# The tail of a PEER layer: another order of its tiles, partial sums kept on chip, and finer steps of routing

## The chip, the cores and the metric

The kernel runs on one core of one Trainium2 chip. The metric is the device time of one execution in microseconds (us). The times of three runs and one profiled execution are given; all rows come from the profiled one.

## What the kernel computes

The reference is one decoder block for 1024 tokens of width 1024: two gated branches and an output projection (dense matmuls), and then PEER, a mixer over 16384 experts of one neuron each. Only the second part matters here, cut from the reference:

```
q = einsum('btd,dq->btq', h, w_q).reshape(B, T, 8, 2, 128)
v1, i1 = top_k(q[..., 0, :] @ keys1.T, 16)
v2, i2 = top_k(q[..., 1, :] @ keys2.T, 16)
...
top_s, pos = top_k(v1 + v2 of all 16 x 16 pairs, 16)
idx = (i1 * 128 + i2) at pos
g = softmax(top_s)
a = gelu(sum over d of h * expert_down[idx])
y = sum over the 8 heads and 16 entries of g * a * expert_up[idx]
```

The block's output is x + gate2 * y, normalised.

## The kernel before, in words

**Halves and blocks.** The tokens are worked in two halves of 512, and the expert part in eight blocks `b` of 128 tokens: 0 to 3 are half 1, 4 to 7 half 2. For each half the dense groups (`group`, `stream`) run first; at its end come the output projection (`w_out_part`) and the four quarters of the query projection (`w_q`). Each quarter `q` gives the scores of two heads, their best eight entries (`s_part`, `tops`) and the number of each head's best expert (`rank`, L1463).

**Routing.** `route` (L317) makes the gates and expert numbers of one quarter; `gates` (L202) is its softmax. `pack_half` (L284) joins a half's quarters into a list in memory, `tsh_d` (written at L312 and L313). `rare` (L367) picks out the few (token, head) pairs that need more than eight entries and builds one extra list for each half, called block 8 or 9 (`NBLK`, `NBLK + 1`). These three are generators. They stand in the queue `qr`, and each `pump` runs one of them to its next `yield`. In the dense part `step()` pumps `qr` by `rate["r"]` for every k step of a group. In the tail, one pump goes with each expert tile.

**Expert tiles.** A tile is 128 gathered rows of the table `tab`, each 2048 numbers: an expert's down and up vectors. There are two kinds.

- A best-entry tile, (b, j) with j from 0 to 7, holds the best expert of head j for each of the 128 tokens of block b. It needs no list, only `dix` of its quarter. `direct_list` (L487) gathers it, `direct_dot` (L491) multiplies it by the block's rows h2 on VectorE and makes a diagonal weight `Wd`.
- A list tile, j from 8 to 17, holds 128 entries of the block's list. `entry_list` (L500) selects them with two matmuls on `th` and `tl` (the list read back at L477 and L478, `load_block`) and gathers the rows (L483). `entry_dot` (L529) brings h2 to the entries by matmuls with `hh` and `hl`, the two halves of a split of h2 (L472, L473), and makes the weight `W`.

Both end in `add_rows` (L552), which sums the tile into the accumulator `acc` of its block: two matmuls, four pieces in the trace (L556). Item j = 18, the rare row (`rare_rows`, L569), adds the block's share of the rare list's result, which went to memory as `yr_d` (`rare_keep`, L577) and is loaded again for each block. `finish` (L595) loads x2, adds and normalises. The blocks of half 1 have their best entries summed elsewhere (`direct_rows`).

**Order.** `peer_stream` (L693) writes out the list `todo` of all 132 items by calls of `seg`. In half 2 it is:

```
for b, n in EARLY:                      # (5, 4), (6, 4), (7, 8)
    seg(b, range(n))
seg(BH, range(last - AH), False)        # block 4, j = 0 to 10
seg(NBLK + 1, range(PH, PH + NTR[1]))   # rare list of half 2, 6 tiles
todo.extend((BH, j) for j in range(last - AH, last + 1))
...
for b in range(BH + 1, NBLK):           # blocks 5, 6, 7: what is left
    seg(b, range(done.get(b, 0), last + 1))
```

The heads of 5, 6 and 7 are interrupted sums: `rows_keep` (L687) writes them to memory (`y_d`), and `finish` loads and adds them. For each item, `fill` gathers up to `ahead` items further on, `dots` makes the product of the next item, and the item's sum follows. In the dense part (stage 1, one pool in `use`, `ahead` 2) the queue `qp` gives `peer_stream` 0.42 to 0.65 of an item per step. In the tail (two pools, `ahead` 7, nine buffers of gathered rows) it runs item after item. A scheduler then orders each engine's instructions; the order of `todo` is their priority.

**Buffers.** `peer_pools` (L435) takes the number of buffers of `hh` and `hl` as `hb`: 1 in the dense part and 2 in the tail. `rowp` holds three rows of 4 KB in each partition. Two accumulators, `pa` and `pa1`, exist in the tail. h2 rows of half 2 go through two buffers (`load_h2`, L456).

Of the kernel before, what the change touches and what calls it, by code (L numbers as in the profile page):

```python
# [47 lines left out]
REST = 0  # L48
# [8 lines left out]
EARLY = ((5, 4), (6, 4), (7, 8))  # L57
# [26 lines left out]
def block_kernel(ctx: ExitStack, tc: tile.TileContext, x, xT, cT, w_ada, b_ada, b_adaT, n1T, w_inp, w_alr,  # L84
# [62 lines left out]
    y_d = [dram.tile([P, D], F32, name=f"y_d{b}") for b in range(NBLK)]  # L147
# [54 lines left out]
    def gates(pool, ts, H, n, tag):  # L202
        dd = pool.tile([P, H, n], F32, name="dd" + tag)
        nc.vector.tensor_tensor(dd, ts, ts[:, :, 0:1].to_broadcast([P, H, n]), op=OP.subtract)
        nc.scalar.activation(dd, dd, AF.Exp)
        sm = pool.tile([P, H], F32, name="sm" + tag)
# [110 lines left out]
    def route(hf, q, tsel, tv, ti):  # L317
        K1, R = KS - 1, 2 * BH
        if q == 0:
            for i in range(BH):  # L320
                nc.scalar.activation(tsel[:, i, 3 * NCS:3 * NCS + 2], lane1.to_broadcast([P, 2]), AF.Identity,
                                     bias=lane0(hf * BH + i) - 1.0)
        cand = r2.tile([P, R, NCAND], F32, name="cand")
# [43 lines left out]
    def rare(gi, rps):  # L367
# [48 lines left out]
        dd, sm = gates(r2, ts, 1, TOPK, "q")  # L416
# [152 lines left out]
    def rare_rows(pl, ul, b):  # L569
        gi, bi = GRP[b]  # L570
        y = ul.tile([P, 2 * D], F32, name="yr", tag="uv")
        nc.scalar.dma_start(y[:, :D], yr_d[gi])
        W = pl["pq"].tile([P, P], F32, name="Wr", tag="e2", bufs=pl["ahead"] + 2)
        (nc.vector if pl["own"] else nc.gpsimd).tensor_scalar(W, iota[:, :P], rcol[gi][:, bi:bi + 1], None, op0=OP.is_equal)
        return W, y

    def rare_keep(pl, gi, acc):  # L577
        y = pl["pt"].tile([P, 2 * D], F32, name="yk", tag="uv")
        nc.scalar.activation(y[:, :D], acc, AF.Identity)
        nc.scalar.dma_start(yr_d[gi], y[:, :D])  # L580

# [105 lines left out]
    def rows_keep(b, acc):  # L687
        y = rowp.tile([P, D], F32, name="yd", tag="row")
        nc.scalar.activation(y, acc, AF.Identity)
        nc.scalar.dma_start(y_d[b], y)  # L690
        summed.add(b)

    def peer_stream():  # L693
        last = PH + NT
        todo, opens, closes = [], {}, {}

        def seg(b, js, close=True):
            opens.setdefault((b, js[0]), len(opens))
            todo.extend((b, j) for j in js)
            if close:  # L700
                closes[b, js[-1]] = True
# [21 lines left out]
        def lists(k):  # L723
            pl = use[-1]
            b, j = todo[k]
            if j < PH:
                if (b, j) in opens:
# [849 lines left out]
```

## Time and profile before

| | us |
|---|---|
| median of three runs | 1624.85 |
| lowest, highest | 1624.53, 1633.76 |
| the profiled execution | 1630.22 |
| its span, first to last instruction | 1628.1 |
| mean granted clock of TensorE | 0.937 |

Engines are PE (TensorE; PEld is its weight load), DVE (VectorE), ACT (ScalarE), POOL (GpSimd) and SP; ACTq and POOLq are the issuing side of ACT and POOL. A clock of 1.00 is 2.4 GHz, and what is below is a mean of that and 1.2 GHz. Times within a profile are us from the start of the span. In rows of groups, busy time in us and the mean in ns stand behind the first bar, idle time of the engine just before these instructions and what ended it behind the second.

### The profile page before, as it was taken

To read this page: it belongs to the slowest core of one execution; us is meant where nothing else is said; L and a number is where in the kernel's file an instruction comes from. 1 tells how busy PE (TensorE), PEld (TensorE's weight loads), DVE (VectorE), ACT (ScalarE), POOL (GpSimd) and SP (SyncE) were. 2 spreads that over 40 slices of the span, in tenths; PEclk is the share of its full clock that TensorE was granted. 3 is DMA by queue.
4 is the path that set the end of the run, shared out by engine and by line. 5 is a ranking of instruction groups with operands and counts; after the bars stand their busy time and mean duration, and the time that the engine had idled before them with its cause. 6 is when DMAs were issued, how large, how long until landed. Compare 5 with 4: busy or idle time off the path is not lost. (4 is left out here: it accounts for less than half of the span.)

```text
span 1628.1 us, 20186 instructions
## 1 busy us (share of the span) xinstructions
PE 1429.0 (88%) x6076; PEld 1073.5 (66%) x6076; DVE 1081.8 (66%) x2766; ACT 774.0 (48%) x1684; POOL 822.0 (50%) x677
## 2 busy tenths in 40 slices
PE   5999989999998898898988899998879985688984
PEld 3777757888768776686766667776668762354542
DVE  7664653111455699968787878778888757666763
ACT  4553333333445464735444665556455445354531
POOL 4331247543375455645675787654766454133331
PEclk7999989999999998899999999999999998879997
DMA  9643633324377556647756777957866588688992
GB/s 312 231 142 113 188 121 113 95 78 145 108 243 255 167 170 221 242 125 263 262 199 216 283 263 279 348 183 233 298 248 227 201 285 321 229 334 350 419 361 87
DMA packets 124200, 364.64 MB, mean 224 GB/s; under 512 B 16857, under 2 KB 27353, under 8 KB 108210
## 3 DMA queue, kind: packets, MB, share of 16 engines
q0 software_dynamic: 30336, 175.39, 29.1%
q1 hardware_dynamic: 70272, 132.15, 24.9%
q10 hardware_dynamic: 23474, 55.73, 9.5%
q8 instruction: 49, 0.80, 0.2%
q14 instruction: 69, 0.57, 0.1%
HBM read 336.27 MB, written 26.95 MB: 223 GB/s over the span
## 5 line engine op out<-in xcount | busy, mean ns | idle before, releaser
L1101 POOL TENSOR_TENSOR wl<-wt,wh 128x512 fp32r<-128x512 f32 x257 | 371.3, 1451 | 368.2 <-ACT wh L1099 332.0
L180 PE MATMUL mm<-wl,hTh 128*128 128x512 f32 x896 | 365.0, 407 | 9.0 <-DVE wl L1101 6.0
L1099 ACT ACTIVATE wh<-wt 128x512 fp32r<-128x512 f32 x368 | 228.4, 626 | 285.2 <-PE mm L181 164.8
L179 PE MATMUL mm<-wh,hTh 128*128 128x512 f32 x896 | 342.4, 412 | 22.3 <-DVE q L1222 5.1
L181 PE MATMUL mm<-wh,hTl 128*128 128x512 f32 x896 | 359.8, 405 | 0.2 <-DVE hTl L1058 0.2
L179 PEld LDWEIGHTS mm<-wh,hTh 128*128 128x128 f32 x896 | 172.5, 194 | 72.1 <-ACT wh L1099 6.7
L1101 DVE TENSOR_TENSOR wl<-wt,wh 128x512 fp32r<-128x512 f32 x111 | 106.3, 958 | 162.6 <-ACT wh L1099 155.2
L180 PEld LDWEIGHTS mm<-wl,hTh 128*128 128x128 f32 x896 | 173.3, 193 | 55.2 <-DVE wl L1101 9.4
L181 PEld LDWEIGHTS mm<-wh,hTl 128*128 128x128 f32 x896 | 172.5, 193 | 41.6 <-issue 1.4
L179 PE MATMUL mm<-hTh,wh 128*128 128x512 f32 (+1 forms) x448 | 169.0, 380 | 9.0 <-ACT vt L1146 4.6
L483 POOL DMA_INDIRECT uv<-in_tab_dram,ix x92 | 99.4, 1081 | 141.3 <-ACT ix L514 40.8
L180 PE MATMUL mm<-hTl,wh 128*128 128x512 f32 (+1 forms) x448 | 168.0, 376 | 1.2 <-DVE hTl L176 1.2
L181 PE MATMUL mm<-hTh,wl 128*128 128x512 f32 (+1 forms) x448 | 160.5, 372 | 2.2 <-POOL wl L1101 1.2
L537 DVE SCALAR_TENSOR_TENSOR uv<-uv,hps 128x512 f32<-128x512 f32 x144 | 95.5, 683 | 34.4 <-PE hps L536 18.5
L565 DVE SCALAR_TENSOR_TENSOR vl<-uv,r,vh 128x512 fp32r<-128x512 f32 x92 | 90.8, 1019 | 40.5 <-ACT vh L564 35.6
L179 PEld LDWEIGHTS mm<-hTh,wh 128*128 128x128 f32 x448 | 87.1, 195 | 25.3 <-ACT vt L1146 7.3
L181 PEld LDWEIGHTS mm<-hTh,wl 128*128 128x128 f32 x448 | 86.8, 195 | 18.1 <-POOL wl L1101 2.3
L180 PEld LDWEIGHTS mm<-hTl,wh 128*128 128x128 f32 x448 | 87.7, 196 | 16.0 <-DVE hTl L176 1.9
L556 PE MATMUL acc<-uv,W 128*128 128x512 f32 x184 | 92.3, 626 | 1.8 <-ACT W L549 1.8
L535 PE MATMUL hps<-hh,E 128*128 128x512 f32 x144 | 74.1, 515 | 22.3 <-DVE uv L537 14.4
L556 PE MATMUL acc<-uv,Wd 128*128 128x512 f32 x128 | 64.9, 647 | 23.3 <-ACT Wd L497 21.3
L952 DVE SCALAR_TENSOR_TENSOR adacc<-wada,sc,adacc 128x1024 f32<-128x1024 f32 x28 | 41.3, 1476 | 32.9 <-DMA wada<-in_w_ada_dram 32.7
(950 smaller groups left out, 2629.0 us busy)
## 6 DMA issues: line engine op xcount, KB each, us to landing
wt<-in_w_inp_dram SPq DMA_DIRECT2D x224, 256.0 KB
wt<-in_w_qp_dram SPq DMA_DIRECT2D x80, 256.0 KB
wada<-in_w_ada_dram SPq DMA_DIRECT2D x32, 512.0 KB
wt<-in_w_outp_dram SPq DMA_DIRECT2D x64, 256.0 KB
wada<-in_w_ada_dram SPq DMA_DIRECT2D x32, 256.0 KB
s_d<-so ACTq DMA_DIRECT2D x32, 256.0 KB
xr<-in_x_dram ACTq DMA_DIRECT2D x8, 512.0 KB
x_d<-x ACTq DMA_DIRECT2D x8, 512.0 KB
```

The source lines that it names most:

```text
L179: nc.tensor.matmul(ps, lh, rh, start=first, stop=False)
L180: nc.tensor.matmul(ps, lh, rl, start=False, stop=False)
L181: return nc.tensor.matmul(ps, ll, rh, start=False, stop=last).ins
L483: nc.gpsimd.indirect_dma_start(out=uv[:], out_offset=None, in_=tab, in_offset=bass.IndirectOffsetOnAxis(ap=ix, axis=0))
L535: nc.tensor.matmul(hps, Ej, hh[:, sl], start=True, stop=False)
L537: nc.vector.scalar_tensor_tensor(uv[:, sl], uv[:, sl], 1.0, hps, op0=OP.mult, op1=OP.mult, accum_out=r[:, 2 + n:3 + n])
L556: nc.tensor.matmul(acc[:, sl], W, v[:, sl], start=first, stop=last)
L565: nc.vector.scalar_tensor_tensor(vl, v, r[:, 5:6], vh.bitcast(F32), op0=OP.mult, op1=OP.subtract)
L952: nc.vector.scalar_tensor_tensor(acc, wt, sc[:, k:k + 1], acc, op0=OP.mult, op1=OP.add)
L1099: nc.scalar.activation(wh, wt, AF.Identity)
L1101: eng.tensor_tensor(wl, wt, wh.bitcast(F32), op=OP.subtract)
```

## The change

- **Order.** `EARLY` is now (5, 0 to 3), (6, 0 to 3), (7, 0 to 5); block 4's first six best-entry tiles follow. Then `LATER`: (5, 4 to 7), (6, 4 to 7), (7, 6 and 7), and block 4 from j = 6 to 17. Only then come the rare list, the lists of blocks 5 and 6, block 4's rare row, and block 7. Items up to block 4's sixth (`stage1`) may run in the dense part.
- **Kept on chip.** `rows_keep` holds the interrupted sums of 5, 6 and 7 in `rowp` (the second part is added on VectorE) and that of block 4 in `ph`; `y_d` serves half 1 only. The result of half 2's rare list stays in `yrk` and is used from there by the four rare rows.
- **Folded ahead.** `rare_rows` loads x2 and, on GpSimd, multiplies the kept sum by `g2row` and adds it to x2, so that `finish` multiplies the accumulator and adds.
- **Accumulators.** They alternate (`turn`, `held`) in place of going by even and odd blocks.
- **h2** is released after a run of best-entry tiles and loaded again for the next.
- **Routing.** `route` yields twice at its start, after heads 3 and 7, and in `gates`; `rate["r"]` is 1.3 from the end of half 1 on, where it was 1.0 until the end of half 2.
- **`hb`** of the tail is 1.

```diff
-EARLY = ((5, 4), (6, 4), (7, 8))
+EARLY = ((5, 0, 4), (6, 0, 4), (7, 0, 6))
+LATER = ((5, 4, 8), (6, 4, 8), (7, 6, 8))
...
         nc.scalar.activation(dd, dd, AF.Exp)
+        yield
...
+        for _ in range(2):
+            yield
         cand = r2.tile([P, R, NCAND], F32, name="cand")
...
-            if h == 3:
+            if h % 4 == 3:
                 yield
...
-        dd, sm = gates(r2, ts, R, KS, "")
+        dd, sm = yield from gates(r2, ts, R, KS, "")
...
-        nc.scalar.dma_start(y[:, :D], yr_d[gi])
+        if not pl["own"]:
+            nc.scalar.dma_start(y[:, :D], yr_d[gi])
...
-        return W, y
+        if not pl["own"]:
+            return W, y
+        nc.scalar.dma_start(y[:, D:], x2_d[b])
+        kept["fin", b] = y
+        if b in kept:
+            nc.gpsimd.tensor_tensor(kept[b], kept[b], late["g2row"], op=OP.mult)
+            nc.gpsimd.tensor_tensor(y[:, D:], y[:, D:], kept[b], op=OP.add)
+        return W, kept["rare"]
 
     def rare_keep(pl, gi, acc):
+        if pl["own"]:
+            kept["rare"] = pl["ph"].tile([P, D], F32, name="yrk")
+            nc.scalar.activation(kept["rare"], acc, AF.Identity)
+            return
...
+    def rows_keep(pl, b, acc):
+        if b in kept:
+            nc.vector.tensor_tensor(kept[b], kept[b], acc, op=OP.add)
+            return
+        kept[b] = rowp.tile([P, D], F32, name="yb", tag="row") if b > BH else pl["ph"].tile([P, D], F32, name="yb")
+        nc.scalar.activation(kept[b], acc, AF.Identity)
...
     def finish(pl, b, acc, part=False):
-        t2b = pl["pt"].tile([P, 2 * D], F32, name="fin", tag="uv")
+        ready = ("fin", b) in kept
+        t2b = kept.pop(("fin", b)) if ready else pl["pt"].tile([P, 2 * D], F32, name="fin", tag="uv")
         y, x3 = t2b[:, :D], t2b[:, D:]
-        nc.scalar.dma_start(x3, x2_d[b])
+        if not ready:
+            nc.scalar.dma_start(x3, x2_d[b])
...
-        for b, n in EARLY:
-            seg(b, range(n))
-        done = dict(EARLY)
-        seg(BH, range(last - AH), False)
+        for b, j0, j1 in EARLY:
+            seg(b, range(j0, j1))
+        seg(BH, range(6), close=False)
+        stage1 = len(todo)
+        for b, j0, j1 in LATER:
+            seg(b, range(j0, j1))
+        seg(BH, range(6, last), open_=False)
         seg(NBLK + 1, range(PH, PH + NTR[1]))
-        todo.extend((BH, j) for j in range(last - AH, last + 1))
-        closes[BH, last] = True
         for b in range(BH + 1, NBLK):
-            seg(b, range(done.get(b, 0), last + 1))
+            if b == NBLK - 1:
+                seg(BH, (last,))
+            seg(b, rows)
...
+                if todo[k + 1] != (b, j + 1):
+                    del h2s[b]
...
-                if len(use) == 1 and b >= BH and b != NBLK and (j >= PH or (1, j // 2) not in topped):
+                if len(use) == 1 and b >= BH and b != NBLK and (nxt >= stage1 or (1, j // 2) not in topped):
...
-                odd = len(use) > 1 and (b >= NBLK or b % 2)
-                accs[b] = use[-1]["pa1" if odd else "pa"].tile([P, D], F32, name="acc")
+                turn = 0 if len(use) == 1 else 1 - turn
+                if turn in held:
+                    turn = 1 - turn
+                held[turn] = b
+                accs[b] = use[-1]["pa1" if turn else "pa"].tile([P, D], F32, name="acc")
...
-            rate["r"] = RA2 if hf else RA
+            rate["r"] = RA2
...
-    use.append(peer_pools("1", "left", UVB, 2, 2, AH, EB, True))
+    use.append(peer_pools("1", "left", UVB, 1, 2, AH, EB, True))
```

## Rows read from the trace of the kernel before

**Rows 1.** Stretches: us, PE, PEld, DVE, ACT, POOL busy (count), clock, DMA share, GB/s.
```profile
0.00:1347.00 1347.00, 1220.08 (x5469) 961.25 (x5470) 903.35 (x2049) 658.00 (x1323) 741.62 (x598) 0.95 0.61 208
1347.00:1402.00 55.00, 38.43 (x108) 18.35 (x106) 37.69 (x154) 25.77 (x69) 15.91 (x16) 0.88 0.81 308
1402.00:1440.00 38.00, 18.78 (x52) 11.76 (x51) 25.64 (x166) 15.31 (x47) 12.14 (x14) 0.65 0.52 192
1440.00:1606.00 166.00, 151.73 (x452) 82.19 (x452) 111.54 (x398) 73.73 (x245) 49.44 (x49) 0.95 0.89 359
1500.00:1550.00 50.00, 47.70 (x151) 26.05 (x149) 38.09 (x128) 24.89 (x82) 19.96 (x20) 1.00 1.02 420
```

**Rows 2.** Timeline of POOL, the gathers of half 2: start, us, instruction.
```profile
1272.63 0.96 POOL L483 DMA_INDIRECT uv<-in_tab_dram,dix  x1 [3.48 <-PE acc L566]
...
1346.99 0.93 POOL L483 DMA_INDIRECT uv<-in_tab_dram,dix  x1 [0.30 <-issue]
1358.66 0.94 POOL L483 DMA_INDIRECT uv<-in_tab_dram,dix  x1 [10.74 <-DVE ti L193]
...
1381.64 1.50 POOL L483 DMA_INDIRECT uv<-in_tab_dram,dix  x1 [0.78 <-PE aux L297]
...
1402.41 0.95 POOL L483 DMA_INDIRECT uv<-in_tab_dram,ix  x1 [16.17 <-ACT ix L514]
...
1430.69 0.96 POOL L483 DMA_INDIRECT uv<-in_tab_dram,ix  x1 [5.14 <-ACT ix L514]
...
1586.45 0.94 POOL L483 DMA_INDIRECT uv<-in_tab_dram,ix  x1 [5.90 <-PE hps L536]
```

**Rows 3.** Timeline of ACT's issuing side: the list written and read back.
```profile
1385.06 0.54 ACTq L312 DMA_DIRECT2D tsh_d<-th  x1
...
1397.41 0.32 ACTq L477 DMA_DIRECT2D thl<-tsh_d  x1
```

**Rows 4.** Timeline of PE: the first list sum, and the first after the rare chain.
```profile
1410.54 3.29 PE L556 MATMUL acc<-uv,W 128*128 128x512 f32 x4
...
1442.96 3.78 PE L556 MATMUL acc<-uv,W 128*128 128x512 f32 x4 [0.91 <-ACT W L549]
```

**Rows 5.** The chain that ended last: start, us, what.
```profile
1557.30 3.20 PE acc L556 x4
...
1597.90 1.72 PE acc L556 x4
...
1600.08 5.59 PE acc L556 x12
...
1605.70 1.23 DVE fin L602
1607.00 2.35 POOL fin L603
```

**Rows 6.** Waits from 440 to 1347 us: total us, times, longest.
```profile
PE aux L1480 <- ACT qt L1433: 12.9, 3, 6.5
```

**Rows 7.** Groups of instructions from 1347 us to the end.
```profile
L556 PE MATMUL acc<-uv,Wd 128*128 128x512 f32 x96 | 49.8, 663 | 21.0 <-ACT Wd L497 19.8 <-ACT yd L689 1.1
...
L603 POOL TENSOR_TENSOR fin<-fin,g2row 128x1024 f32<-128x1024 f32 x3 | 7.0, 2349 | 14.0 <-DVE fin L602 14.0
...
L473 DVE TENSOR_TENSOR hl<-h2l,hh 128x1024 fp32r<-128x1024 f32 x5 | 6.1, 1217 | 7.3 <-ACT hh L472 7.3
L472 ACT ACTIVATE hh<-h2l 128x1024 fp32r<-128x1024 f32 x5 | 5.3, 1057 | 9.4 <-DMA h2l<-h_d 5.8 <-DMA h2l<-h_d,rtok 2.0 <-PE hps L535 1.6
```

**Rows 8.** DMA issues of the whole span, each of 512 KB.
```profile
yr<-yr_d ACTq DMA_DIRECT2D x8, 512.0 KB
...
y_d<-yd ACTq DMA_DIRECT2D x7, 512.0 KB
fin<-y_d ACTq DMA_DIRECT2D x7, 512.0 KB
```

More of the change, by code (lines that the diff above doesn't have):

```diff
@@ L47 @@
 WT = 4
-REST = 0
 RD = 0.62
@@ L146, in block_kernel @@
     yr_d = [dram.tile([P, D], F32, name=f"yr_d{g}") for g in range(NG)]
-    y_d = [dram.tile([P, D], F32, name=f"y_d{b}") for b in range(NBLK)]
+    y_d = [dram.tile([P, D], F32, name=f"y_d{b}") for b in range(BH)]
     ncs_of = [NCS] * NBLK + [TOPK] * NG
@@ L415, in rare @@
         tsel = r2.tile([P, 3 * TOPK + 2], F32, name="qtsel")
-        dd, sm = gates(r2, ts, 1, TOPK, "q")
+        dd, sm = yield from gates(r2, ts, 1, TOPK, "q")
         nc.vector.tensor_tensor(sm, sm, tt[:, n + 2:n + 3], op=OP.mult)
@@ L580, in rare_keep @@
         nc.scalar.dma_start(yr_d[gi], y[:, :D])
+    kept = {}
+    def rows_keep(pl, b, acc):
[4 more added lines that the diff above has]
+        nc.scalar.activation(kept[b], acc, AF.Identity)
     late = {}
@@ L685, in direct_rows, with seg @@
             yield
[L687 to L691, printed above, removed]
     def peer_stream():
         last = PH + NT
-        todo, opens, closes = [], {}, {}
-        def seg(b, js, close=True):
-            opens.setdefault((b, js[0]), len(opens))
+        todo, opens, closes, runs = [], set(), set(), set()
+        def seg(b, js, open_=True, close=True):
+            if open_:
+                opens.add((b, js[0]))
+            if js[0] < PH:
+                runs.add((b, js[0]))
             todo.extend((b, j) for j in js)
             if close:
-                closes[b, js[-1]] = True
+                closes.add((b, js[-1]))
         rows = range(PH, last + 1)
@@ L706, in peer_stream @@
             seg(b, range(0 if b not in summed else PH, last + 1))
-        for b, n in EARLY:
-            seg(b, range(n))
-        done = dict(EARLY)
-        seg(BH, range(last - AH), False)
+        for b, j0, j1 in EARLY:
[5 more added lines that the diff above has]
+        seg(BH, range(6, last), open_=False)
         seg(NBLK + 1, range(PH, PH + NTR[1]))
-        todo.extend((BH, j) for j in range(last - AH, last + 1))
-        closes[BH, last] = True
         for b in range(BH + 1, NBLK):
-            seg(b, range(done.get(b, 0), last + 1))
+            if b == NBLK - 1:
+                seg(BH, (last,))
+            seg(b, rows)
+        held, turn = {}, 0
         h2s, preps, ents, es, accs, wvs = {}, {}, {}, {}, {}, {}
@@ L726, in lists @@
             if j < PH:
-                if (b, j) in opens:
+                if (b, j) in runs:
                     h2s[b] = load_h2(b)
                 ents[k] = direct_list(pl, slot(k), b, j, h2s[b])
+                if todo[k + 1] != (b, j + 1):
+                    del h2s[b]
                 return
@@ L793, in peer_stream, with run @@
             elif lst and j < last:
-                rows_keep(b, accs[b])
+                rows_keep(use[-1], b, accs[b])
             elif lst:
                 finish(use[-1], b, accs[b], b in summed)
-                if len(use) == 1:
-                    for _ in range(REST):
-                        yield
+            if lst:
+                held = {t: c for t, c in held.items() if c != b}
             yield
+    def run(gen):
+        while True:
+            try:
+                next(gen)
+            except StopIteration as e:
+                return e.value
     def peer_rest(pl, pg_):
@@ L826, in peer_rest @@
                     tops16(tv[:, a // 2, a % 2], ti[:, a // 2, a % 2], st[:, a])
-                sels = select16(pg_, tv, ti, PH, "g")
-                while True:
-                    try:
-                        next(sels)
-                    except StopIteration as e:
-                        ts, sel = e.value
-                        break
-                dd, sm = gates(pg_, ts, PH, TOPK, "g")
+                ts, sel = run(select16(pg_, tv, ti, PH, "g"))
+                dd, sm = run(gates(pg_, ts, PH, TOPK, "g"))
                 nc.vector.tensor_tensor(dd, dd, sm.unsqueeze(2).to_broadcast([P, PH, TOPK]), op=OP.mult)
```

## The prediction

> **What bounds the kernel now.** I read the stretches of the span first, then the issues of one queue, then the chain at the end. Up to about 1347 us the dense matmuls run, with TensorE 90% busy [rows 1]. Nearly all of the change lies behind that: the tail, in which the expert tiles of half 2 are gathered and summed. The reader should see three stages there, in the same rows. From 1347 to 1402 DMA is at 0.81. From 1402 to 1440 both DMA (0.52) and TensorE (18.8 of 38 us, granted clock 0.65, so much of it at the lower of its two levels, 1.2 GHz) are half idle. From 1440 to 1606 both are nearly full (0.89, and 152 of 166 us). Where DMA is saturated it moves 420 GB/s at 1.02.
>
> So the tail is bound by TensorE and DMA together, with a hole in the middle. The gathers show where the hole comes from. After 1346.99 POOL waits 10.7 us for the ranking of the last quarter (DVE ti), because the next tile in the written order, (7, 6), needs it [rows 2]. After 1381.64 nothing is gathered until 1402.41: the best-entry tiles at hand are used up, and lists need the routing of half 2. Three list gathers follow, then the rare batch is next in the order and its own routing chain lasts until 1430.69. The list itself is written at 1385.06 and read back at 1397.41 [rows 3]. The first list sum is at 1410.54, the steady run starts at 1442.96 [rows 4].
>
> **The change part by part.**
>
> *Stage 1, dense.* The pumping rates of the stream are unchanged, so it stands at the same tile (about 60 of 132) when the dense part ends, and 14 of the 32 best-entry gathers of half 2 are issued by 1347; the first and the last of the 14 are in [rows 2]. The finer steps put waits of ACT for DVE apart from the copies behind them. What they could give back is TensorE's 12.9 us behind the copy of qt, 6.5 us of it in one piece [rows 6]. The same reordering can open as much elsewhere. Bounds -13 and +13 us; I take 0, since those three waits are a tenth of the 127 us in which TensorE was not busy up to 1347 [rows 1], and nothing says which others move. The faster pace in half 1 changes nothing: 32 steps at 1.3 are 41 pumps for some 25 steps of routing.
>
> *Order in the tail.* 24 best-entry sums are left at 1347 (96 pieces, four to a sum [rows 7]); before, 16 of them ran before the lists and 8 among them. Now all 24 run first, and ten of their 18 gathers need no last quarter. So the stall behind DVE ti and the hole after 1381 both have work. Bytes: 18 gathers of 128 rows of 8 KB are 18.9 MB, five loads of h2 2.6, scores and lists 1.6: 23.1 MB, at 420 GB/s 55 us, until 1402. TensorE needs 24 x 1.72 = 41 us [rows 5], DVE, whose product takes as long as the 1.22 us of hl [rows 7], 29 us beside its routing, so DMA sets this. The lists are ready at 1402 too. Their gathers queue behind full rings, so I put the first list sum at 1415, between 1410 (as before) and 1430 (the list read stands behind all best-entry tiles in ACT's order, and the hole moves instead).
>
> *Lists.* From there 46 list tiles and 4 rare rows remain. In a run of nothing but lists, from 1557.30 to 1600.08, 14 lists and one rare row took 42.8 us; with 1.72 for the row that is 2.93 each [rows 5]. 46 x 2.93 + 4 x 1.72 = 142 us. Before, 1440 to 1606 held 43 lists and 12 light sums, 147 us by the same prices, in 166: 19 idle. The rare chain, 28 us from 1402 to 1430, now lies beside ten lists (29 us). The second copy of hh and hl goes; a handover costs 1.06 us on ACT and 1.22 on DVE [rows 7] after the last product of the old block, beside two or three sums of 1.72 that are still queued: 0 to 2.3 us, four times. I take 10 us of idle for all this, between 0 and 19. End of sums: 1415 + 152 = 1567.
>
> DMA has the same stretch for 46 gathers, 48.2 MB, plus 4 h2, 4 x2, 4 outputs and lists, 7.0 MB: 55 MB, 131 us. On-chip keeping takes away three writes and three reads of y_d and one write and four reads of yr_d [rows 8], 5.8 MB, and the five reloads of h2 give 2.6 back: net 3 MB, 7.6 us of a full DMA, contained in the sums above. The fold on POOL, 2.35 us for the product [rows 7] and taken alike for the sum, comes before later gathers on POOL and waits for the x2 row; nine buffers of gathered rows cover it. If they don't, four blocks times 5 us is 20 us.
>
> *The end.* The last block now does the product with the sum's row on DVE and needs no POOL product of 2.35 us at 1607.00: 2.4 us of the 22.4 that follow 1605.70 [rows 5].
>
> Sum: 1567 + 20.0 = 1587 of span, against 1628.1. That is 41 us less. The profiled execution took 1630.2 us and the median is 1624.85; the difference carries over: 1624.85 - 41 = **1584 us**.
>
> **A rule to weigh.** DMA moved 420 GB/s from 1500 to 1550 us, at 1.02 [rows 1]. The Trainium skill (DMA: Bandwidth & Descriptors, Bandwidth, "Where 436 GB/s comes from") says that for transfers between HBM and SBUF the memory side holds a core to some 358 GB/s. The row doesn't agree: a whole 50 us lies above it. By the rule, an estimate, the 78 MB of the tail would take 219 us and end near 1566 without any idle time, so transfers alone would set the tail; that is the second rival below, which I price by a row.
>
> **The rivals.**
>
> *The hole moves* (0.14). The list read stays where the written order puts it, behind best-entry tiles whose gathers are late; before, ACT read the list 12 us after it was written. For: ACT also stood 5.8 us for loads of h2 in the tail [rows 7]. Against: the order of the engines is not that of the code alone. First list sum at 1430 instead of 1415: 1599 us.
>
> *Transfers bind* (0.10). The tail can't hold 420 and gets the mean of the last stretch, 359 [rows 1]. 78.3 MB / 359 = 218 us, gathers done at 1565; the last gather came 19 us before the last sum's end (1586.45 [rows 2] to 1605.70), so 1584 + 20 = 1604 of span, 1601 us.
>
> *The order doesn't reach the engines* (0.08). The gathers wait for nine buffers, and if the sums are as late as before, the new order fills nothing; only the bytes and the end remain, 7.6 + 2.4: 1615 us.
>
> *Slower: one buffer for hh* (0.08). With one copy, the next block's hh can't be written before the last product of the old one. If its conversion stands in ACT's queue where the list is made, seven tiles early, every weight copy behind it waits, and the pipeline drains: up to 7 x 2.93 = 20.5 us at each of four handovers, 82 us; 1584 + 82 = 1666. It decides the sign from two full handovers on. Against it: half 1 already runs with one copy, and hh L472 waited 1.6 us for PE in the tail [rows 7].
>
> **How the numbers follow.** The forecast has 0.60, with its own range 1566 to 1600 (idle 0 to 19, first list 1410 to 1422, dense -13 to +13, not all at once). A measurement of this kernel can tell about 1%, 16 us: faster means below 1608.6. Forecast and the first two rivals lie there, 0.84; the third is no change, 0.08; the fourth slower, 0.08. The range leaves out the last two: 1562 to 1610.
>
> **What would show it.** Right: POOL's gathers run from 1347 to about 1395 with no gap over 5 us; 24 best-entry sums come before the first list sum, which lies at 1410 to 1422; 50 sums follow in 142 to 161 us; no stretch like that of 1402 to 1440 with a granted clock of 0.65; no POOL product between the last sum and the last square. Wrong: a gap of 15 us in the gathers with idle DMA, waits of ACT or DVE at each block's first list, or a dense part that ends over 10 us from 1347.

## The result and the profile after

The changed kernel took 1619.14 us (median of 16 runs, 1614.26 to 1623.05) where the kernel before took 1628.07 in the same comparison: ratio 0.9939, interval 0.9925 to 0.9953. That is 9 us less instead of 41, no change by the bound of 1%, and outside the range. The profiled execution took 1623.05 us, its span was 1621.0.

Stretches of the changed kernel, columns as in [rows 1]:

```profile
0.00:1347.00 1347.00, 1214.43 (x5445) 957.17 (x5446) 905.71 (x2044) 655.32 (x1315) 735.26 (x597) 0.95 0.61 206
1347.00:1402.00 55.00, 40.22 (x116) 20.16 (x115) 36.74 (x152) 26.28 (x72) 22.89 (x23) 0.88 0.94 376
1402.00:1440.00 38.00, 25.02 (x58) 11.27 (x56) 31.55 (x122) 16.34 (x51) 17.82 (x13) 0.87 0.78 299
1440.00:1602.00 162.00, 146.31 (x462) 82.20 (x460) 118.88 (x451) 76.79 (x248) 53.43 (x50) 0.97 0.82 317
```

The stretch from 1402 to 1440 is no longer half idle: DMA rose from 0.52 to 0.78, TensorE from 18.8 to 25.0 us, its granted clock from 0.65 to 0.87. From 1347 to 1402 DMA rose from 0.81 to 0.94, but TensorE did hardly more, 40.2 us against 38.4. So more was transferred early, and hardly more was summed early.

Timeline of POOL, the gathers of half 2 and the operations between them, to set beside [rows 2]:

```profile
1354.27 0.94 POOL L486 DMA_INDIRECT uv<-in_tab_dram,dix  x1 [0.30 <-issue]
1367.07 1.96 POOL L486 DMA_INDIRECT uv<-in_tab_dram,dix  x1 [11.87 <-PE acc L559]
...
1371.54 0.94 POOL L486 DMA_INDIRECT uv<-in_tab_dram,dix  x1 [1.26 <-PE acc L559]
...
1382.04 1.92 POOL L486 DMA_INDIRECT uv<-in_tab_dram,dix  x1 [7.19 <-DVE g L347]
...
1403.53 0.96 POOL L486 DMA_INDIRECT uv<-in_tab_dram,dix  x1 [0.15 <-issue]
1406.94 2.39 POOL L584 TENSOR_TENSOR yb<-yb,g2row 128x1024 f32<-128x1024 f32 x1 [2.45 <-DVE yb L601]
...
1431.79 0.98 POOL L486 DMA_INDIRECT uv<-in_tab_dram,ix  x1 [5.84 <-ACT vq L245]
...
1449.96 0.94 POOL L486 DMA_INDIRECT uv<-in_tab_dram,ix  x1 [0.77 <-ACT ix L517]
1467.98 0.96 POOL L486 DMA_INDIRECT uv<-in_tab_dram,ix  x1 [17.08 <-PE tps L509]
```

There are four long gaps. Two lie in the best-entry gathers, where the forecast had none over 5 us: after 1354 POOL waits 11.9 us for a sum to free a buffer, and from 1372 to 1382 no tile is gathered either (the profile puts 7.2 us of that down to the routing on DVE). From 1404 to 1432 the first list isn't ready, and from 1450 to 1468 the rare batch isn't. Before, these last two stood at 1382 to 1402 and, after three list gathers, up to 1431 [rows 2].

Timeline of ACT, the list written and read back, block 4's h2 row loaded again and converted, and the list's entries (`ts`) copied, to set beside [rows 3]:

```profile
1401.95 0.54 ACTq L313 DMA_DIRECT2D tsh_d<-th  x1
...
1413.36 0.32 ACTq L462 DMA_DIRECT2D h2l<-h_d  x1
...
1418.30 0.33 ACTq L480 DMA_DIRECT2D thl<-tsh_d  x1
...
1421.58 0.33 ACTq L481 DMA_DIRECT2D tll<-tsh_d  x1
1422.78 1.06 ACT L475 ACTIVATE hh<-h2l 128x1024 fp32r<-128x1024 f32 x1 [2.56 <-DMA h2l<-h_d]
1427.97 0.20 ACT L497 ACTIVATE rd<-rd 128x1 f32<-128x1 f32 x1 [4.12 <-DVE uv L496]
...
1428.84 0.29 ACT L511 ACTIVATE ts__12636<-tps 128x170 f32<-128x170 f32 x1
```

Timeline of PE, the first selection of list entries, the last best-entry sum and the first list sum, to set beside [rows 4]:

```profile
1424.47 0.33 PE L509 MATMUL tps<-tll,E 128*128 128x112 f32 x2
...
1433.29 2.60 PE L559 MATMUL acc<-uv,Wd 128*128 128x512 f32 x4
...
1440.77 1.54 PE L559 MATMUL acc<-uv,W 128*128 128x512 f32 x3
```

The order did reach TensorE: all best-entry sums stand ahead of the first list sum. But that sum is at 1441, not 1415. The list is written 17 us later than before and read 16.4 us after it was written, instead of 12.4. The last two of these timelines show one more delay: TensorE has selected the first entries by 1424.8, but ACT copies them only at 1428.84, behind a step of a best-entry tile (`rd`) that waited 4.1 us for its product on DVE.

Timeline of the end, to set beside [rows 5]:

```profile
1599.69 1.88 PE L559 MATMUL acc<-yrk,Wr 128*128 128x512 f32 x4
1601.61 1.22 DVE L631 TENSOR_TENSOR yr<-acc,g2row 128x1024 f32<-128x1024 f32 x1 [4.88 <-PE acc L559]
1602.93 1.23 DVE L632 TENSOR_TENSOR yr<-yr 128x1024 f32<-128x1024 f32 x1
1604.19 1.06 ACT L634 ACTIVATE yr<-yr 128x1024 f32<-128x1024 f32 x1 [6.38 <-DVE yr L632]
```

POOL's product is gone from the path, and 19.4 us follow the last sum instead of 22.4.

### The profile page after: what moved, and what is told of

It reads as the page before. It is cut to its first block, busy times and chain, and to the rows that moved or that the text cites. A ratio compares the mean times of both kernels' runs of the same rounds, so it can differ in the third digit from the quotient of the medians.

```text
span 1621.0 us, 20193 instructions
## 1 busy us (share of the span) xinstructions
PE 1426.0 (88%) x6076; PEld 1070.8 (66%) x6076; DVE 1096.4 (68%) x2769; ACT 775.9 (48%) x1685; POOL 830.0 (51%) x682
## 2 busy tenths in 40 slices
DMA packets 123338, 361.49 MB, mean 223 GB/s; under 512 B 16763, under 2 KB 27259, under 8 KB 107348
## 4 chain that ended last, share of the span: by engine, by line
PE 46%; DVE 21%; DMA 16%; issue 7%; ACT 5%; POOL 4%; ACTq 0%; SPq 0%; DVEq 0%; POOLq 0%
PE mm L179 10%; PE mm L180 10%; PE mm L181 10%; PE acc L559 5%; DMA uv<-in_tab_dram,ix 4%; DMA wada<-in_w_ada_dram 3%; DMA uv<-in_tab_dram,dix 2%; POOL wl L1133 2%; DMA uvd<-in_down_dram,dix 2%; DVE uv L540 2%; PE hps L538 1%; DVE wl L1133 1%; PE hps L539 1%; DVE vl L568 1%; DMA wt<-in_w_outp_dram 1%
## 5 line engine op out<-in xcount | busy, mean ns | idle before, releaser
L1133 POOL TENSOR_TENSOR wl<-wt,wh 128x512 fp32r<-128x512 f32 x257 | 366.7, 1434 | 376.9 <-ACT wh L1131 342.2
L486 POOL DMA_INDIRECT uv<-in_tab_dram,ix x92 | 100.5, 1093 | 140.5 <-PE hps L539 31.1
L180 PEld LDWEIGHTS mm<-hTl,wh 128*128 128x128 f32 x448 | 86.7, 193 | 15.4 <-DVE hTl L176 1.9
L559 PE MATMUL acc<-uv,W 128*128 128x512 f32 x184 | 88.8, 606 | 2.0 <-ACT W L552 1.9
L559 PEld LDWEIGHTS acc<-uv,Wd 128*128 128x128 f32 x128 | 26.0, 213 | 57.5 <-ACT Wd L500 29.7
```

What stands on the lines that cost most here:

```text
L180: nc.tensor.matmul(ps, lh, rl, start=False, stop=False)
L486: nc.gpsimd.indirect_dma_start(out=uv[:], out_offset=None, in_=tab, in_offset=bass.IndirectOffsetOnAxis(ap=ix, axis=0))
L559: nc.tensor.matmul(acc[:, sl], W, v[:, sl], start=first, stop=last)
L1133: eng.tensor_tensor(wl, wt, wh.bitcast(F32), op=OP.subtract)
```

## The experiments

Dense parts differ from run to run, so for each profiled execution I count from its dense end (end of the last copy of qt, ACT L1465, here 1351.61 + 1.57 = 1353.2): to the first list sum, and to the end of the last sum of all, which I call the tail's length. The comparisons ran on several chips, on which the kernel before took 1627 to 1635 us. The ratio takes that out only as far as a slower chip slows all parts alike, so I read ratio and tail together.

| run | median us | ratio, interval | dense end | first list sum | tail | rest |
|---|---|---|---|---|---|---|
| before | 1628.07 | 1 | 1346.6 | +63.9 | 259.1 | 22.4 |
| after | 1619.14 | 0.9939 (0.9925-0.9953) | 1353.2 | +87.6 | 248.4 | 19.4 |
| after_again | 1618.61 | 0.9942 (0.9922-0.9963) | 1343.7 | +89.3 | 250.4 | 19.3 |
| a_rr4 | 1615.00 | 0.9929 (0.9902-0.9955) | 1343.2 | +95.6 | 250.6 | 19.1 |
| a_rr99 | 1615.50 | 0.9928 (0.9906-0.9949) | 1345.9 | +95.6 | 250.3 | 19.1 |
| a_sp | 1629.14 | 0.9995 (0.9972-1.0019) | 1359.3 | +99.6 | 251.5 | 18.2 |
| a_steps0 | 1622.58 | 0.9966 (0.9945-0.9987) | 1345.7 | +98.1 | 261.2 | 19.3 |
| a_order0 | 1620.33 | 0.9957 (0.9934-0.9981) | 1353.3 | +59.5 | 246.8 | 19.4 |
| c_hh | 1619.76 | 0.9944 (0.9924-0.9963) | 1344.8 | +88.2 | 255.0 | 19.3 |
| c_hh_sp | 1628.97 | 1.0011 (0.9991-1.0032) | 1355.6 | +89.8 | 251.7 | 19.4 |
| c_hh_rr4 | 1632.74 | 1.0020 (1.0002-1.0037) | 1346.8 | +100.5 | 260.2 | 19.3 |
| c_rare | 1614.98 | 0.9884 (0.9857-0.9910) | 1346.1 | +92.4 | 250.2 | 18.2 |
| c_rare_rr4 | 1617.85 | 0.9906 (0.9881-0.9931) | 1350.6 | +94.6 | 252.0 | 18.2 |
| c_hh_spt_rare | 1615.02 | 0.9888 (0.9866-0.9910) | 1348.5 | +83.9 | 246.8 | 18.2 |
| c_order0_rare | 1617.71 | 0.9914 (0.9883-0.9945) | 1350.6 | +64.2 | 243.0 | 19.4 |
| c_nofold | 1608.92 | 0.9839 (0.9810-0.9869) | 1348.1 | +86.7 | 240.6 | 21.4 |
| c_fold_dve | 1614.29 | 0.9891 (0.9859-0.9922) | 1345.4 | +88.3 | 246.3 | 20.0 |
| c_rare_nofold | 1612.56 | 0.9863 (0.9835-0.9890) | 1347.4 | +88.7 | 241.7 | 21.2 |
| c_hh_spt_rare_nofold | 1607.76 | 0.9841 (0.9813-0.9868) | 1342.4 | +86.3 | 240.3 | 21.5 |
| c_order0_nofold | 1610.17 | 0.9903 (0.9876-0.9929) | 1346.5 | +59.1 | 236.7 | 21.2 |

The forecast in these terms: first list sum at 1415 - 1346.6 = +68.4, tail 1567 - 1346.6 = 220.4, rest 20.0.

**More routing steps per tile.** First theory: one pump of routing per tile in the tail makes the list late.

```diff
-RR = 1.0
+RR = 4.0     # a_rr4
+RR = 99.0    # a_rr99
```

> Four routing steps of half 2 are pumped per tile in the tail instead of one; the rest as in the changed kernel. Theory (routing stands between best-entry tiles in the in-order queues of DVE, ACT and PE, so the list is late): the list, written at 1402 us in the changed kernel, is written near 1390, the first list sum moves from 1441 to about 1429, and the time falls by 8 to 15 us from 1619. Rival (the tail after 1441 is bound by DMA or by the folds on POOL): the first list sum may move, but the end stays, within 4 us of 1619. Rival (only the finer steps cost): no change, since they stay.

> All routing steps of half 2 are issued ahead of the tail's tiles, otherwise the changed kernel. Theory (queue order): ranking to list takes the 17 us it took in the kernel before, list written near 1385, first list sum near 1418, time 12 to 25 us below 1619; the price is that best-entry products wait some us behind the routing. Rival (the end is bound by DMA or folds): within 4 us of 1619. Rival (best-entry products that wait behind routing hold the gather buffers, so the hole moves once more): 1615 to 1630.

The theory fell. Timeline of ACT in a_rr99, the last quarter's scores copied, ranked and written as a list:

```profile
1346.60 1.09 ACT L1514 ACTIVATE so<-aux 128x512 f32<-128x512 f32 x2 [0.69 <-PE aux L1512]
...
1361.78 0.58 ACT L1514 ACTIVATE so<-aux 128x512 f32<-128x512 f32 x1
...
1365.96 0.26 ACT L329 ACTIVATE tif<-ti 128x64 f32<-128x64 uint32 x1 [2.60 <-DVE ti L193]
...
1395.97 0.54 ACTq L313 DMA_DIRECT2D tsh_d<-th  x1
```

The list is written 50.1 us after the dense end of 1345.9, against 48.8 in the changed kernel: what looked like an earlier list was an earlier dense end. The 15 us between the second and the third copy of scores stand in the changed kernel too (1353.86 and 1369.14). All routing was issued ahead in the code, and it made no difference to where it ran.

**List reads on SP's queue.**

```diff
-        nc.scalar.dma_start(th.bitcast(F32), ts_d[b][:, :3 * n + 2])
-        nc.scalar.dma_start(tl.bitcast(F32), ts_d[b][:, 3 * n + 2:])
+        nc.sync.dma_start(th.bitcast(F32), ts_d[b][:, :3 * n + 2])
+        nc.sync.dma_start(tl.bitcast(F32), ts_d[b][:, 3 * n + 2:])
```

> The two reads of each list are issued by SP's queue instead of ACT's, otherwise the changed kernel. Rival to the order theory (the read behind best-entry weight copies on ACT is what makes the list late): the read moves from 1418 to about 1405 plus the time that the write takes to land, 1414, the first list sum falls by 4 to 10 us, the time by as much. Theory (the list is late already when it is written at 1402, and the write's landing sets the first read): under 4 us from 1418, time 1615 to 1620.

Both missed. The read went out 7.7 us after the write (1401.41 against 1393.75) and the first list gather at 1420.29, yet the first list sum came later, at +99.6, with hh of block 4 converted only at 1446.56. The dense end moved to 1359.3, and in this profile most of the lost time lies there; c_hh_sp below, with the same reads on SP in the dense part too, ends it at 1355.6, and no other run ends it behind 1353.3. From 1100 to 1347 TensorE had 212.8 us of work here, 221.5 in a_rr4, but also only 214.6 in the first profile of the changed kernel, so how SP's queue does this stays open:

```profile
1100.00:1347.00 247.00, 212.77 (x995) 165.60 (x994) 182.95 (x491) 127.61 (x273) 141.60 (x117) 0.94 0.68 232
```

**Coarse steps.**

```diff
-        for _ in range(2):
-            yield
...
-            if h % 4 == 3:
+            if h == 3:
...
-        dd, sm = yield from gates(r2, ts, R, KS, "")
+        dd, sm = run(gates(r2, ts, R, KS, ""))
```

> The added yields in route and in the gates are taken out again (steps as coarse as before); order, buffers, on-chip sums and the rate of half 1 stay. Theory (order of the tail, one pump per tile): fewer pumps are needed from ranking to list, some 2 to 3 of about 12, so the first list sum comes 4 to 8 us earlier, 1433 to 1437; time 1611 to 1617. Rival (the finer steps alone cost what was lost, through the dense part that ends 5 to 7 us later and through the list): dense end back at 1347, first list sum near 1415, time near 1595. Rival (the finer steps help the dense part): time 1620 to 1630.

Missed by theory and by the rival that blamed the steps: the list is no earlier, and the tail is 11 us longer (261.2). The dense end, 1345.7, lies inside the spread. The time without them, 1622.6 instead of 1619, lies in the last rival's range, but it is the tail and not the dense part that grew. The finer steps are no cost; by this they help, by some 4 us.

**The old order back.**

```diff
-EARLY = ((5, 0, 4), (6, 0, 4), (7, 0, 6))
-LATER = ((5, 4, 8), (6, 4, 8), (7, 6, 8))
+EARLY = ((5, 0, 4), (6, 0, 4), (7, 0, 8))
-        seg(BH, range(6), close=False)
-        stage1 = len(todo)
-        for b, j0, j1 in LATER:
-            seg(b, range(j0, j1))
-        seg(BH, range(6, last), open_=False)
+        stage1 = len(todo) + 6
+        seg(BH, range(last))
-            seg(b, rows)
+            seg(b, range({c: n for c, _, n in EARLY}[b], last + 1))
```

> Only the order of the tail is put back: the best-entry tiles 4 to 7 of blocks 5 and 6 stand with their blocks again, behind the lists of block 4; on-chip sums, early folds, one buffer for hh, finer steps and the rest stay. Theory (best-entry tiles that wait for gathers stand ahead of the list's steps in the in-order queues): the first list sum falls from 1441 to 1410 to 1420, and what the new order itself was worth shows in the time; if it was worth nothing, 1612 to 1622, since later light sums of 1.72 us are the same work at another place. Rival (the new order is what gains, by 10 us or more): 1626 to 1636. Rival (the handover with one buffer for hh, or the folds, cost more than the order): above 1630.

This is the run that decides. Timelines of ACT and PE of a_order0, list written, list read, first list sum:

```profile
1387.29 0.54 ACTq L312 DMA_DIRECT2D tsh_d<-th  x1
...
1397.92 0.32 ACTq L479 DMA_DIRECT2D thl<-tsh_d  x1
...
1412.77 2.54 PE L558 MATMUL acc<-uv,W 128*128 128x512 f32 x4
```

From the dense end the list is written at +34.0, read at +44.6 and summed at +59.5, against +48.8, +65.1 and +87.6 in the changed kernel. So it is the new order, not the steps nor their rate, that puts best-entry tiles between the steps of the list. And the second half of the expectation holds too: a first list sum 28 us earlier doesn't shorten the tail by more than 2 to 4 us. The stretches of a_order0:

```profile
1347.00:1402.00 55.00, 37.00 (x108) 18.34 (x107) 39.96 (x152) 27.97 (x72) 23.07 (x20) 0.88 0.80 301
1402.00:1440.00 38.00, 30.49 (x94) 16.98 (x92) 29.48 (x179) 18.26 (x59) 11.60 (x13) 0.91 0.78 309
1440.00:1600.00 160.00, 141.17 (x420) 77.34 (x418) 110.48 (x386) 71.85 (x234) 56.53 (x52) 0.93 0.83 322
```

TensorE is idle 18.0 + 7.5 + 18.8 = 44.3 us here, and 14.8 + 13.0 + 15.7 = 43.5 us in the changed kernel's three stretches. The old hole is closed in a_order0 as well (30.5 of 38 us), although the order of best-entry tiles is the old one: what closes it must be another part of the change. I take it to be the rare batch, which now comes behind all lists of block 4; no run shows that alone. At its old place the rare batch interrupts the lists of block 4, which takes two copies of hh.

**Block 4's h2 kept and split ahead.** The reload of h2 at 1413 and hh at 1423 seemed to be what holds the list besides its read.

```diff
...
+    def split_h2(pl, b, h2):
+        hh = pl["ph"].tile([P, D], F32R, name="hh")
+        hl = pl["ph"].tile([P, D], F32R, name="hl")
+        nc.scalar.activation(hh, h2, AF.Identity)
+        nc.vector.tensor_tensor(hl, h2, hh.bitcast(F32), op=OP.subtract)
+        early[b] = hh, hl
...
-        seg(BH, range(6), close=False)
-        stage1 = len(todo)
+        seg(BH, range(PH), close=False)
+        stage1 = len(todo) - 2
...
-        seg(BH, range(6, last), open_=False)
+        seg(BH, range(PH, last), open_=False)
...
+                if (b, j) == (BH, PH - 1):
+                    split_h2(pl, b, h2s[b])
```

> Block 4's tiles 6 and 7 come first of the late best-entry tiles, so that the block's h2 row is not loaded a second time (13 loads become 12), and its hh and hl are made right there, ahead of the late tiles; the rest as in the changed kernel. Theory now: the first list sum waits for two things in a row of the queues, the list read on ACT and h2 of block 4, reloaded at 1413 and turned into hh at 1423. If h2 ends last, the first list sum comes 8 to 12 us earlier, 1429 to 1433, time 1607 to 1612; if the list's steps on PE behind best-entry sums end last, under 4 us, 1615 to 1620.

> As c_hh, and the lists are read by SP's queue. With ACT's queue alone the list reads went earlier (1401 instead of 1418) and the first list gather too (1420 instead of 1432), but hh came only at 1447 and the first list sum at 1459. Theory (both waits, each hides the other): with both taken away the first list sum is at 1422 to 1430, time 1600 to 1609. Rival (what holds is the order of PE's queue, whatever feeds it): first list sum above 1436, time 1615 to 1630.

> As c_hh, with four routing steps per tile instead of one. Theory (routing and h2 each delay the list): list written near 1390, first list sum at 1420 to 1428, time 1598 to 1607. Rival (only one of them counts, the gains don't add): as the better of the two alone, 1607 to 1615. Rival (end bound by DMA or folds): 1612 to 1620 although the first list sum is earlier.

c_hh_sp has the reads on SP's queue besides, c_hh_rr4 the four routing steps. All three missed their better theory. c_hh left the first list sum where it was (+88.2). c_hh_sp had its first list gather at 1413 and DMA at 1.01 from 1402 to 1440, and still its first list sum at +89.8; right behind, the rare batch stopped the gathers for 23 us. c_hh_rr4 was the slowest of all (+100.5, tail 260.2). (The early list reads that the second of these expectations quotes are those of a_sp, on SP's queue.) Here the waits traded places. I take it that what was made early pushed something else back in the same queues; no run follows that step by step.

**The rare batch one block later.**

```diff
-        seg(NBLK + 1, range(PH, PH + NTR[1]))
         for b in range(BH + 1, NBLK):
+            if b == BH + 2:
+                seg(NBLK + 1, range(PH, PH + NTR[1]))
             if b == NBLK - 1:
                 seg(BH, (last,))
-            seg(b, rows)
+                seg(BH + 1, (last,))
+            seg(b, rows if b > BH + 1 else range(PH, last))
```

> The rare batch of half 2 stands one block later, behind the lists of block 5 instead of those of block 4, and block 5's rare row moves to where block 4's stands; the rest as in the changed kernel. Theory (there are two holes, the first list and the rare batch; the rare one showed a gap of 17 us in the gathers at 1450 and 5 to 6 us of TensorE idle from 1470 to 1480): the gap goes, the list run takes 154 to 157 us instead of 161, time 1612 to 1616. Rival (the gathers catch up by themselves, the nine buffers cover the gap): 1618 to 1621. Rival (the rare chain's steps, now beside the lists of block 5, cost the same there): 1618 to 1625.

> As c_rare, with four routing steps per tile. Theory (four steps per tile gained 4 us because the rare chain ended earlier, not by the first list sum, which stood at 1439): with the rare batch out of the way nothing is left for it, time as c_rare, 1611 to 1616. Rival (the four steps gain on the list's side): 4 us below c_rare.

> Block 4's h2 kept and split ahead (c_hh), list reads on SP's queue in the tail alone, and the rare batch one block later. With c_hh and SP the list gathers went out from 1413 and DMA stayed at 1.01 up to 1440, but then the rare batch stopped the gathers for 23 us. Theory (both holes have to go together, then the forecast's order pays): no gap over 6 us in the gathers, first list sum at 1425 to 1435, time 1594 to 1606. Rival (while best-entry tiles run, DMA sets the pace and the lists' own work on TensorE is all that is left behind them, so the order can't pay): time 1612 to 1622 although no gap is left.

> The old order of the best-entry tiles (a_order0) with the rare batch one block later. In a_order0 TensorE was idle 7.3 us between 1440 and 1480, around the rare batch. Theory (the rare batch's wait is a hole of its own, whatever the order of the best-entry tiles): time 1612 to 1616 against 1620. Rival (nothing is gained since later idle stretches grow): 1618 to 1624.

In c_rare the gap at 1450 is gone: from 1440 to 1480 TensorE has 39.1 of 40 us of work, and the list run takes 157.8 us instead of 161. But a gap of 12.4 us opens at 1537, in front of block 7. Ratio and median say a gain of 4 to 9 us, the tail says none; I take the rare batch for a few us and no more. c_rare_rr4 added nothing, as its theory had it. c_hh_spt_rare (c_hh and c_rare, with `rq = nc.sync if len(use) > 1 else nc.scalar` as the queue of the list reads, so on SP in the tail alone) still had a first list sum at +83.9. Its time, 1615.02, lies in its rival's range, but gaps of 24, 10 and 14 us were left in its gathers, so the condition of neither theory was met and neither is tested. c_order0_rare has a tail 4 us shorter than a_order0, and its time, 1617.71, lies between its two theories.

**No fold ahead.** Reading the list run of the changed kernel, I found DVE operations that took several times their usual time. Timelines of DVE and of POOL, two such places, two usual durations of the same lines, and the product that follows:

```profile
1522.73 3.05 DVE L660 TENSOR_SCALAR E<-ea,hw 128x256 fp32r<-128x256 f32 x1 [1.11 <-PE hps L539]
...
1526.92 1.22 DVE L476 TENSOR_TENSOR hl<-h2l,hh 128x1024 fp32r<-128x1024 f32 x1
...
1559.72 3.13 DVE L476 TENSOR_TENSOR hl<-h2l,hh 128x1024 fp32r<-128x1024 f32 x1
...
1563.17 4.00 DVE L632 TENSOR_TENSOR yr<-yr 128x1024 f32<-128x1024 f32 x1
...
1569.29 1.21 DVE L632 TENSOR_TENSOR yr<-yr 128x1024 f32<-128x1024 f32 x1
1570.42 0.67 DVE L540 SCALAR_TENSOR_TENSOR uv<-uv,hps 128x512 f32<-128x512 f32 x1
```

```profile
1523.26 2.37 POOL L585 TENSOR_TENSOR yr<-yr,yb 128x1024 f32<-128x1024 f32 x1
...
1559.39 2.37 POOL L585 TENSOR_TENSOR yr<-yr,yb 128x1024 f32<-128x1024 f32 x1
...
1563.70 2.38 POOL L585 TENSOR_TENSOR yr<-yr,yb 128x1024 f32<-128x1024 f32 x1
```

Each ends at the end of a POOL fold, or there plus about its own time: 1525.78 against 1525.63, 1562.85 against 1561.76, 1567.17 against 1566.08. Six operations after 1347, each over a fold, took 13.7 us more than the same lines in c_nofold, the run without folds below (the expectation of that run counts 10.9). Where TensorE pays for it shows behind the last two. It waits 4.9 us, its longest wait in the list run, for the product at 1570.42, which stood behind them on DVE:

```profile
1571.15 0.80 PE L538 MATMUL hps<-hh,E 128*128 128x512 f32 x1 [4.94 <-DVE uv L540]
```

Two variants tell what that costs:

```diff
-        if b in kept:
-            nc.gpsimd.tensor_tensor(kept[b], kept[b], late["g2row"], op=OP.mult)
-            nc.gpsimd.tensor_tensor(y[:, D:], y[:, D:], kept[b], op=OP.add)
...
+        elif ready and b in kept:
+            nc.vector.tensor_tensor(y, kept[b], acc, op=OP.add)
+            nc.vector.tensor_tensor(y, y, g2row, op=OP.mult)
```

c_fold_dve keeps the fold ahead and has nc.vector in place of nc.gpsimd in its two lines.

> No fold ahead: POOL's eight operations (sum so far times the row, plus the x2 row) go, and the end of a block does sum, product and sum on DVE, 1.22 us more per block there; the rest as in the changed kernel. Theory (a POOL operation of 2.4 us holds up DVE operations beside it: 10.9 us of lengthened DVE operations in the tail): DVE gains 10.9 less 4.9 us, the list run takes 155 to 158 us instead of 161, the end after the last sum 1.2 us more; time 1613 to 1618. Rival (the lengthened DVE operations lie where TensorE had work, so they cost nothing): 1619 to 1622, and the 1.2 us at the end show.

> The same fold ahead, but on DVE: 2.4 us of DVE per block, none on POOL; the rest as in the changed kernel. Theory (POOL holds DVE up for as long as its operation takes): DVE loses as much as before, so the time stays, 1616 to 1621, while the DVE operations of 3 to 4 us in place of 0.3 to 1.2 vanish. Rival (only the place of the fold in POOL's queue ahead of gathers costs): 1610 to 1615. Rival (work on POOL is free and DVE is the busy one): 1622 to 1630.

> c_rare and c_nofold together. If the two causes in the list run are different ones, their gains add: c_rare measured 0.988 of before, c_nofold should take another 2 to 5 us, 0.985 to 0.987, about 1606 to 1611 us where before takes 1631. Rival (the handover to the next block, not the fold, is what is left): as c_rare, 0.988.

> All of it: h2 of block 4 kept and split ahead, list reads on SP in the tail, the rare batch one block later, no fold ahead. Theory (causes add): 0.983 to 0.986 of before, 1603 to 1608 us where before takes 1631. Rival (list start and list run trade off against each other, as c_hh showed, which gained nothing by itself): as c_rare_nofold, 0.985 to 0.988. The forecast's 0.975 isn't expected by either, since in all runs so far TensorE has 36 to 42 us of work in the 55 us from 1347 to 1402, while DMA is at 0.94 or more.

c_nofold is 10 us below the changed kernel by the median, 16 by the ratio, and 8 to 10 by the tail; of these 7 are in the list run (154.0 us instead of 161). TensorE's work there is the same, 145 us; its idle time falls from 15.3 to 8.7. One lengthened operation is left, by 0.8 us, which stands beside no fold in the changed kernel either. The end pays 2.0 us (21.4 instead of 19.4), some more than the 1.2 expected. The kernel before took 1634.75 us in this comparison and 1628.07 in the changed kernel's, so I trust the tail more than the ratio here. Three more pairs in the table differ by the folds alone: their tails are 10.1 us shorter without (a_order0), 8.5 (c_rare) and 6.5 (c_hh_spt_rare), their medians 10.2, 2.4 and 7.3 us lower. In the timeline of c_nofold the operations of the same lines show their usual durations:

```profile
1551.76 1.22 DVE L632 TENSOR_TENSOR yr<-yr 128x1024 f32<-128x1024 f32 x1
...
1553.50 1.22 DVE L476 TENSOR_TENSOR hl<-h2l,hh 128x1024 fp32r<-128x1024 f32 x1
```

c_fold_dve lies between: DVE does the 2.4 us per block itself, nothing is lengthened beside a fold, and it gained 5 us by the median, 8 by the ratio and 2 to 4 by the tail. That is better than the theory had it and in the range of its first rival, which blamed the fold's place among POOL's gathers. But an account of DVE alone gives the same: 13.7 us of lengthening go, and eight operations of 1.22 us come, 3.9 us less. In c_nofold 13.7 go and three operations of 1.22 come before the last sum, 10.0 less, where the tail gained 8 to 10. In the list run of the changed kernel no DVE product waited for a gather, by the profile. So the rival isn't needed, though no run excludes a small share for it. The other two show that the gains don't add: c_rare_nofold and c_hh_spt_rare_nofold are no better than c_nofold alone within their intervals, though the latter, at 0.9841, has the lowest median of the study (1607.76). (The 0.94 of DMA that its expectation gives to all runs holds for the new order only roughly, with 0.88 in a_sp, and not for the old one, with 0.80 in a_order0.)

**The order without folds.**

```diff
-LATER = ((5, 4, 8), (6, 4, 8), (7, 6, 8))
...
-            nc.gpsimd.tensor_tensor(kept[b], kept[b], late["g2row"], op=OP.mult)
-            nc.gpsimd.tensor_tensor(y[:, D:], y[:, D:], kept[b], op=OP.add)
```

c_order0_nofold is a_order0 and c_nofold together, as above; after_again has no edit.

> The changed kernel itself, unchanged, once more on the chip of the run beside it. Expected 0.992 to 0.996 of before; its dense part, which has the same instructions in the same order as in the runs with four or all routing steps per tile, should end at 1340 to 1352, the spread of runs seen so far.

> The old order of the best-entry tiles (a_order0) with no fold ahead (c_nofold). If the new order is worth nothing by itself (a list phase that TensorE bounds and a best-entry phase that DMA bounds only change places): as c_nofold, 0.982 to 0.986 of before. If the folds hid its worth: 0.988 to 0.993, near a_order0. If the old order is the better one without folds: below 0.980.

The changed kernel repeated its ratio, 0.9942, with a dense end 9.5 us earlier than in its first profile, from the same instructions. For the order the answers differ. By the ratio the new order is worth 0.6% once the folds are gone (0.9839 against 0.9903, on two chips); by the median 1.3 us; by the tail the old one is 4 us shorter (236.7 against 240.6). The one pair that differs by the order alone and ran on one chip is c_rare and c_order0_rare: 0.9884 against 0.9914 with intervals that overlap, 2.7 us by the median for the new order, and 7 us by the tail for the old. Whether it gains a little or nothing stays open; the 31 us that the forecast gave it (1584 against 1615 in the rival where the order doesn't reach the engines) are in no run.

## Why the prediction was wrong

**Dense, 0 with bounds of 13: held.** The first profile showed a dense end at 1353.2 and seemed to speak against it. The same kernel again showed 1343.7, and before 1346.6.

**The end, 2.4 us: held,** 3.0 measured. **Bytes, net 3 MB: held,** 361.49 MB instead of 364.64, with 13 loads of h2 instead of 8.

**The first list sum at 1415: this step failed.** "The lists are ready at 1402 too" took the list's time from the old order and carried it into the new one. Measured from the dense end it is +87.6 to +89.3 instead of +68.4, 19 to 21 us of the 28 to 30 by which the tail was underestimated. after_again splits it against before: ranking to list 28.8 us instead of 17.2, write to read 16.7 instead of 12.4, read to gather 13.4 instead of 5.0, gather to sum 10.4 instead of 8.1. Best-entry work of the new order stood in front, as at 1428.84 on ACT, and steps of the rare list and folds among it. That a_order0, with the best-entry tiles of blocks 5 and 6 behind the lists again, has +59.5 shows that it is the order. "DMA sets this" failed with it. The transfers were nearly in time: the last best-entry gather went out at 1403.5, 50 us after the dense end. But the last of the 24 sums ended at 1435.9, and they took 52 us of TensorE where I had put 41. I had priced them by the end of the span [rows 5], although [rows 7] already had 49.8 us for them. The rival "The hole moves" named this place, the list read in ACT's order, but with 0.14, and it priced one of four steps: 1430 and 1599 us, where 1433 to 1441 and 1619 were measured.

**That the hole is time to be had, and that the first list sum moves the end one for one: this failed as well,** and it carried the sum. a_order0 has a first list sum 28 us earlier and a tail within 4 us. TensorE's idle time after 1347 was 43.5 us with the one order and 44.3 with the other: what the new order filled at one place it opened at another. With the new order alone it is the same, on a smaller scale: a_rr4 and a_rr99 have their first list sum 6 to 8 us later than the changed kernel and about the same tail, and c_hh_spt_rare has it 8.5 us earlier than c_rare for 3.4 us of tail. I could have seen the bound in [rows 1]: 209 us of TensorE work stood in the tail before, and the change took none of it away, so a tail of 220 us left 11 us for all waits, in a tail that had 50.

**The list run at 152: 9 us short.** Work was 145.5 us where I had 142, and idle time 15.3 where ten us were to hold everything. "Nine buffers cover it" treated the fold as a matter of POOL's queue; what the runs show of its price is on DVE, a term that the forecast put at nothing. Without the folds the run takes 154.0 us, 8.7 of them idle. The bound that I kept for them, 20 us, was for another mechanism and covered the size by luck: 8 to 10 measured by the tail.

The Trainium skill has the rule that I left out (SBUF — State Buffer, "SBUF: two separate sides"): GpSimd and VectorE share a pair of ports under an exclusive lock; whichever starts first holds it for its whole instruction, and the other fully blocks if it needs the pair, as a VectorE operation with two SBUF inputs does. The trace agrees that it blocks: a DVE sum of 1.22 us took 4.00 beside a fold of 2.38. It doesn't show that the first to start wins: the row of that sum begins 0.53 us before the fold's.

**"Transfers bind"** didn't come: from 1440 to 1602 DMA was at 0.82. **"Slower: one buffer for hh"** neither: at 1558.63 the conversion waited 0.35 us for PE's last product.

## What to carry to other kernels

Before giving a hole its full length as a gain, set the work that remains on the busiest engine against the forecast's length of the stage: if the change removes no work there, only idle time can go, and it has to be said which. When filler is moved ahead of a dependent chain, walk that chain through the queue of each engine that the filler uses; here the filler delayed every step from the ranking to the first sum, and the hole came back behind it. An elementwise operation on POOL is not free just because POOL is idle: look at what DVE does in the same microseconds.

## What the runs showed of the hardware

Beside a POOL operation of 2.4 us with two inputs in on-chip memory, some DVE operations ended only when it had ended, or their own time after: 0.35 us became 3.05, 1.22 became 3.13 and 4.00. Not all did: two searches (FIND_INDEX8) at 1423.89 and 1424.15, beside a fold from 1423.59 to 1425.95, took the 0.28 us that they take elsewhere. One kernel, the same instructions: its dense part ended at 1353.2 us in one profiled execution and at 1343.7 in another, a spread larger than most effects studied here. DMA at 0.94 and 0.97 of its time from 1347 to 1402, in the two profiles of the changed kernel, gave TensorE 40.2 and 37.9 us of work, where 0.81 gave it 38.4 before.
